# Query, key and value projections as seven half products per pair of feature blocks, with token sums streamed from DRAM

## The chip, the core and the metric

The kernel runs on one core of a Trainium2 chip. The metric is the device time of one execution in microseconds. TensorE (PE in the rows) multiplies matrices, VectorE (DVE), ScalarE (ACT) and GpSimd (POOL) do elementwise work, and SyncE (SP) issues the DMAs. Every engine works through its own instructions in order and waits on semaphores.

## What is computed

One decoder layer on 1040 tokens (16 learned ones ahead of 1024) of 1024 features. The part that matters here, cut from the reference:

```python
xn = rms_norm(h, mix_pre_g[l])
proj = xn @ w_in[l]                       # z, xbc, dt, q, k, v side by side
q = proj[..., OFF_Q:OFF_K].reshape(Bsz, L, SB_HEADS, SB_HEAD_DIM)
k = proj[..., OFF_K:OFF_V].reshape(Bsz, L, SB_HEADS, SB_HEAD_DIM)
v = proj[..., OFF_V:IN_COLS].reshape(Bsz, L, SB_HEADS, SB_HEAD_DIM)
y_ssd = ssd_mixer(z, xbc, dt_raw, ...)    # a scan over 9 chunks of tokens, 2 groups of heads
y_sb = rms_norm(stick_breaking_attention(q, k, v).reshape(Bsz, L, SB_WIDTH), sb_norm_g[l])
mix = jnp.concatenate([y_ssd, y_sb], axis=-1) @ w_out[l]
h = h + rms_norm(mix, mix_post_g[l])      # then the feed-forward part
```

q, k and v are 1024 features each: 16 heads of 64, taken as 8 pairs of heads, so 8 blocks of 128 features of each kind, 24 in all. Attention takes the pairs one after the other, and for each pair 8 blocks of 128 queries.

## The kernel before

The normed tokens lie transposed in SBUF, features on the partitions: `xs`, in three tiles by token columns (`CH`: 400, 384, 256), each with a high part (a 32-bit format that TensorE reads in one pass) and a low part, the rest. A weight block is loaded (`wr_`, 512 KB), ScalarE rounds it to the high part (`wh_`, L151), GpSimd subtracts for the low part (`wl_`, L152). `project_steps` (L165) then does, for each of three chunks of columns and eight blocks of 128 features, three matmuls: high by high, high by low, low by high. That is 72 matmuls for each of the 24 blocks of q, k and v. ScalarE takes q and v out of PSUM (L382, L394); k is split into high and low by ScalarE and VectorE (L388, L389).

These projections are filler. `qkv_flow` yields half chunks (12 matmuls, in the first pairs whole chunks of 24), and the code that runs the scan of the second group of heads (`scan_steps(1)`) and later the attention loop takes one to a few of them at hand-set places (`FILL`, `run(fill, ...)`). In attention TensorE's order is that of the code; the other engines' orders come from a scheduler. For pair p and query block i the loop does `block_weights` (scores `z` on TensorE, two sigmoids on ScalarE into `kp` and `bt`, a product scan over `kp` on VectorE, L773, the product of `bt` with it on GpSimd, L775), and, three blocks behind, `block_turn` (transposes `tw`, copied to `th`) and `block_mix` (`av`, the product with the values). `kp` has two buffers, `bt` three. PSUM has two banks for projections (`psum_mm`). All loads and stores stand in SP's one queue.

The feed-forward part already does its up-projection as seven half products per two blocks of features, in matmuls of 258 columns (L1304); there the sums on the token side stay in SBUF and those of the weights are made on GpSimd (L1264 to L1268).

Of the kernel before, what the change touches and what calls it, by code (L numbers as in the profile page):

```python
# [9 lines left out]
F32 = mybir.dt.float32  # L10
# [22 lines left out]
CH = [(0, 400), (400, 384), (784, 256)]  # L33
# [8 lines left out]
WB = 3  # L42
PPC = XB * 4 + XB + NFF * 3 + NFF + 8 + 8
# [10 lines left out]
def tile_layer(ctx: ExitStack, tc: tile.TileContext, x, meta, rows, parts,  # L54
# [37 lines left out]
    def const(shape, dt, name):  # L92
# [5 lines left out]
    identb = const([P, P], BF16, "identb")  # L98
    nc.vector.tensor_copy(identb, ident)
    ones = const([P, P], F32, "ones")  # L100
    nc.vector.memset(ones, 1.0)
    tri = const([P, P], F32, "tri")
    nc.gpsimd.affine_select(out=tri, in_=ones, compare_op=ALU.is_ge, fill=0.0,
                            base=0, pattern=[[1, P]], channel_multiplier=-1)
    low = const([P, P], F32, "low")
    nc.gpsimd.affine_select(out=low, in_=ones, compare_op=ALU.is_gt, fill=0.0,
                            base=0, pattern=[[-1, P]], channel_multiplier=1)
    lowr = const([P, P], F32R, "lowr")
    nc.vector.tensor_copy(lowr, low)
    maskb = const([P, P], BF16, "maskb")  # L110
    nc.vector.tensor_scalar(maskb, low, -NEG, NEG, op0=ALU.mult, op1=ALU.add)
# [25 lines left out]
    xsd = [dr.tile([NT + 1, P, 512], F32, name=f"xsd{g}", tag=f"xsd{g}") for g in range(2)]  # L137
    mvd = dr.tile([NM, 8, P], F32, name="mvd", tag="mvd")
# [17 lines left out]
    def project_steps(w, ncol, chunks, evac, name, halves_=False, skip=0):  # L156
        hi, lo = w
        for c0, n in chunks:
            s = skip if c0 == 0 else 0
            acc = psum_mm(f"pj_{name}_{c0}")  # L160
            for k in range(KB):
                if halves_ and k == KB // 2:
                    yield
                for j, (a, b) in enumerate(((hi, 0), (hi, 1), (lo, 0))):
                    mm(acc[:ncol, :n - s], a[:, k, :ncol], xs[c0][:, b, k, s:n],  # L165
                       start=(k == 0 and j == 0), stop=(k == KB - 1 and j == 2))
            evac(acc, c0 + s, n - s)
            yield
# [31 lines left out]
    def x_third(c0, name):  # L200
        n = dict(CH)[c0]
        return xp.tile([P, 2, KB, n], F32R, name=name, tag=f"x{c0}")

    xs = {c0: x_third(c0, f"xs{c0}") for c0, _ in CH}
# [12 lines left out]
    def dt_steps(hl):  # L217
        for c0, n in CH:
            acc = psum_mm(f"pj_dt_{c0}")
            for k in range(KB):  # L220
                for j in range(2):
                    mm(acc[:32, :n], hl[:, k, :], xs[c0][:, j, k, :n],
# [5 lines left out]
    with tc.tile_pool(name="pre", bufs=3, side="right") as pre, \  # L228
# [47 lines left out]
        def turn_x(i):  # L276
            c0, nr = spans[i]
            tps = []
            for hf in range(2):
# [6 lines left out]
                base = max(a for a, _ in CH if a <= c0)  # L286
                h, l = (xs[base][:, j, 4 * hf:4 * hf + 4, c0 - base:c0 - base + nr] for j in range(2))
                tps.append((tp, h, l))
            for tp, h, _ in tps:
                nc.scalar.activation(h, tp[:, :, :nr], AF.Copy)  # L290
            for tp, h, l in tps:
                nc.vector.tensor_tensor(l, tp[:, :, :nr], h.bitcast(F32), op=ALU.subtract)
# [55 lines left out]
    qkv_w = [(src[p], f"{nm}{p}") for p in range(8) for nm, src in (("q", w_q), ("k", w_k), ("v", w_v))]  # L348
    ready = {}

    def weights_of(name, ahead=0):
        n = [nm for _, nm in qkv_w].index(name) + ahead
        if n < len(qkv_w) and qkv_w[n][1] not in ready:
            src, nm = qkv_w[n]
            ready[nm] = load_w(src, P, nm)
        return ready.get(name)

    def qkv_block(name, evac, halves_):
        w = weights_of(name)
        for i, _ in enumerate(project_steps(w, P, CH, evac, name, halves_, M0 * (name[0] == "q"))):  # L360
            if halves_ and i == 1:
                weights_of(name, 1)
            yield
# [3 lines left out]
    def qkv_steps(p, post):  # L367
        q = rp.tile([P, L + 3], F32, tag="rq", name=f"q{p}", bufs=3)
        kh = rp.tile([P, L], F32R, tag="rk", name=f"kh{p}", bufs=3)
        later, vt_ = {}, []  # L370

        def values():
            v = rp.tile([P, NT + 1, P], F32, tag="rv", name=f"v{p}")
            vc = rp.tile([P, P], F32, tag="vc", name=f"vc{p}")
            heads[p][2:] = [v, vc]

        def low_k():
            later["kl"] = rp.tile([P, L], F32R, tag="rkl", name=f"kl{p}", bufs=2)
            heads[p] = [q, (kh, later["kl"]), None, None]

        def ev_q(acc, c0, n):
            nc.scalar.activation(q[:, c0:c0 + n], acc[:, :n], AF.Copy)  # L382

        def ev_k(acc, c0, n):
            if c0 == 0:
                low_k()
            kl = later["kl"]
            nc.scalar.activation(kh[:, c0:c0 + n], acc[:, :n], AF.Copy)  # L388
            nc.vector.tensor_tensor(kl[:, c0:c0 + n], acc[:, :n], kh[:, c0:c0 + n].bitcast(F32), op=ALU.subtract)  # L389

        def ev_v(acc, c0, n):
            if c0 == 0:
                vt_.append(rp.tile([P, L], F32, tag="rt", name=f"vt{p}", bufs=1))
            nc.scalar.activation(vt_[0][:, c0:c0 + n], acc[:, :n], AF.Copy)  # L394

        names = [(f"q{p}", ev_q), (f"k{p}", ev_k), (f"v{p}", ev_v)]
        if p < 7:
            for nm, ev in names:
# [1495 lines left out]
```

## Time and profile before

| what | value |
|---|---|
| median of 3 runs | 1734.75 us (1733.84 to 1738.6) |
| the profiled execution | 1735.83 us, span 1733.7 us |
| granted TensorE clock | 0.995 |
| TensorE busy | 1708.7 us (99%) |
| VectorE busy | 1114.4 us (64%) |
| ScalarE busy | 821.6 us (47%) |
| GpSimd busy | 858.3 us (50%) |
| moved by DMA | 173.87 MB |

A matmul's end is modelled and overlaps the next one's start, so what a matmul costs in a row of them is read from start to start. A busy share is an average over stages: the projections of q, k and v stand in two of them, the second scan and attention.

### The profile page before, as it was taken

The page shows a single profiled execution, that of the slowest core. Times are in us where ns is not written, and L with a number is a line of the kernel's source. Part 1 is how long each engine was busy: PE and PEld are TensorE (multiplying, and loading weights), DVE is VectorE, ACT ScalarE, POOL GpSimd, SP SyncE. Part 2 cuts the span into 40 slices and gives each one's busy share as a digit, 9 for nine tenths or more (in the row PEclk, how much of TensorE's full clock was granted, in tenths as well). Part 3 has the DMA queues.
Part 4 walks back from the last instruction along what each step waited for, and adds up shares of the span by engine and source line. Part 5 has one row for each costly group of instructions (what it writes and reads, how often), then busy time and mean ns, then how long its engine had stood idle before and what let it go on. Part 6 is the DMA issues. An engine that isn't in the chain of part 4 may idle for free. (4 is left out here: it accounts for less than half of the span.)

```text
span 1733.7 us, 28039 instructions
## 1 busy us (share of the span) xinstructions
PE 1708.7 (99%) x11230; PEld 1498.9 (86%) x11230; DVE 1114.4 (64%) x1230; ACT 821.6 (47%) x1370; POOL 858.3 (50%) x645
## 2 busy tenths in 40 slices
PE   7999999999999999999999999999999999999998
PEld 6999889888999998998687778999988888887886
DVE  5752964775676686668531457676666666758777
ACT  5423653545566566567553245433333333343544
POOL 4323663685566576555642124587766777400001
PEclk9999999999999999999999999999999999999999
DMA  4232343231011111112215544233332222395335
GB/s 163 58 113 97 101 130 104 67 104 38 26 38 37 38 31 33 38 50 86 82 50 172 175 165 136 63 117 96 110 100 92 92 91 92 114 330 188 104 112 180
DMA packets 90674, 173.87 MB, mean 100 GB/s; under 512 B 10704, under 2 KB 35816, under 8 KB 90544
## 3 DMA queue, kind: packets, MB, share of 16 engines
q1 hardware_dynamic: 90544, 172.08, 31.0%
q8 instruction: 88, 1.44, 0.3%
q14 instruction: 42, 0.34, 0.1%
HBM read 122.32 MB, written 49.73 MB: 99 GB/s over the span
## 5 line engine op out<-in xcount | busy, mean ns | idle before, releaser
L775 POOL TENSOR_TENSOR bt<-bt,kp 128x256 f32<-128x256 f32 (+7 forms) x128 | 213.2, 1684 | 184.5 <-DVE kp L773 147.7
L773 DVE TENSOR_TENSOR_SCAN kp<-kp,hold 128x272 f32<-128x272 f32 (+7 forms) x128 | 183.4, 1473 | 26.0 <-ACT kp L766 14.1
L1247 POOL TENSOR_TENSOR wlo<-wr,whi 128x1024 fp32r<-128x1024 f32 x43 | 106.2, 2479 | 38.0 <-ACT whi L1246 38.0
L1751 POOL TENSOR_TENSOR fms<-fms 128x1 f32<-128x1 f32 x8 | 2.7, 333 | 223.7 <-DMA ar<-fda 187.5
L766 ACT ACTIVATE kp<-z 128x288 f32<-128x288 f32 (+6 forms) x112 | 82.5, 737 | 52.2 <-PE z L765 27.9
L1246 ACT ACTIVATE whi<-wr 128x1024 fp32r<-128x1024 f32 x43 | 45.6, 1059 | 111.5 <-PE fX L1304 68.3
L165 PE MATMUL pj_v<-xs,wh_v 128*128 128x400 f32 (+2 forms) x384 | 94.9, 334 | 0.0
L1376 DVE SCALAR_TENSOR_TENSOR ga<-gr,pp,ga 128x1024 f32<-128x1024 f32 x44 | 72.3, 1643 | 34.9 <-ACT ga L1369 34.1
L165 PE MATMUL pj_k<-xs,wh_k 128*128 128x400 f32 (+2 forms) x384 | 94.4, 333 | 0.0
L789 ACT ACTIVATE th<-tw 128x1024 f32<-128x1024 f32 (+2 forms) x96 | 75.6, 816 | 38.5 <-PE tw L787 38.4
L165 PE MATMUL pj_q<-xs,wh_q 128*128 128x386 f32 (+2 forms) x384 | 93.8, 331 | 0.0
L165 PE MATMUL pj_X<-xs,wh_X 128*128 128x400 f32 (+2 forms) x384 | 93.1, 330 | 0.0
L1636 ACT ACTIVATE dh<-ar 128x512 fp32r<-128x512 f32 x77 | 48.5, 630 | 92.4 <-PE dnB L1714 44.7
L165 PE MATMUL pj_z<-xs,wh_z 128*128 128x386 f32 (+2 forms) x384 | 91.5, 326 | 0.0
L741 DVE CAST qh<-q 128x128 fp32r<-128x128 f32 x64 | 46.9, 734 | 67.1 <-PE z L765 66.7
L1637 DVE TENSOR_TENSOR dl<-ar,dh 128x512 fp32r<-128x512 f32 x77 | 53.2, 691 | 50.3 <-ACT dh L1636 47.5
L951 PE MATMUL mo<-woa,yh 128*128 128x512 f32 x256 | 85.2, 400 | 0.0
L767 ACT ACTIVATE bt<-z 128x288 f32<-128x288 f32 (+6 forms) x112 | 82.8, 740 | 0.0
L802 PE MATMUL av<-th,v 128*64 128x128 f32 x1152 | 78.1, 280 | 0.0
L787 PE MATMUL tw<-ident,bt 128*128 128x128 f32 x576 | 75.4, 274 | 0.0
L802 PEld LDWEIGHTS av<-th,v 128*64 128x64 f32 x1152 | 62.3, 138 | 14.0 <-issue 11.3
L787 PEld LDWEIGHTS tw<-ident,bt 128*128 128x128 f32 x576 | 65.5, 141 | 5.8 <-issue 2.7
(560 smaller groups left out, 5635.2 us busy)
## 6 DMA issues: line engine op xcount, KB each, us to landing
wr<-in_w_up SPq DMA_DIRECT2D x44, 512.0 KB
fds<-ga SPq DMA_DIRECT2D x44, 256.0 KB
b<-in_w_down SPq DMA_DIRECT2D x44, 256.0 KB
ar<-fds SPq DMA_DIRECT2D x44, 256.0 KB
fda<-ga SPq DMA_DIRECT2D x33, 256.0 KB
ar<-fda SPq DMA_DIRECT2D x33, 256.0 KB
yk<-yd SPq DMA_DIRECT2D x16, 512.0 KB
wor<-in_w_out SPq DMA_DIRECT2D x12, 512.0 KB
```

Of the source, the lines that this page charges most:

```text
L165: mm(acc[:ncol, :n - s], a[:, k, :ncol], xs[c0][:, b, k, s:n], start=(k == 0 and j == 0), stop=(k == KB - 1 and j == 2))
L766: nc.scalar.activation(kp[:, :, a:a + w], z[:, :, :w], AF.Sigmoid, scale=-QSCALE)
L767: nc.scalar.activation(bt[:, :, a:a + w], z[:, :, :w], AF.Sigmoid, scale=QSCALE)
L773: nc.vector.tensor_tensor_scan(kp[:, j][:, ::-1], kp[:, j][:, ::-1], hold[:, L - n:L][:, ::-1], 0.0, op0=ALU.mult, op1=ALU.max)
L775: nc.gpsimd.tensor_tensor(bt[:, j, 0:m], bt[:, j, 0:m], kp[:, j, 1:m + 1], op=ALU.mult)
L787: nc.tensor.transpose(tw[:, j, b, :], bt[:, j, c0:c0 + P], ident)
L789: nc.scalar.activation(th[:, :, :nb, :], tw[:, :, :nb, :], AF.Copy)
L802: mm(av[halves[j], :], v[:, kb, halves[j]], th[:, j, b, :], start=kb == 0, stop=kb == i)
L951: mm(acc, u[:, k, :], v[:, cs], start=(k == 0 and j == 0), stop=(k == 7 and j == 2))
L1247: nc.gpsimd.tensor_tensor(l, raw, h.bitcast(F32), op=ALU.subtract)
L1376: nc.vector.scalar_tensor_tensor(v, self.g[jj][:, :, i:i + 256], fconv_w[:, j, i:i + 1], v, op0=ALU.mult, op1=ALU.add)
L1637: sub(lo[:, k], raw, hi[:, k].bitcast(F32), op=ALU.subtract)
```

## The change

The 24 blocks are taken in 12 pairs (k and q, v and q, k and v, for two head pairs at a time). For a pair, the weights and the tokens are each cut into a two by two arrangement: two feature blocks by two halves of the 1024 input features, and two halves of the input features by two halves of the tokens (520 columns). Seven half products, with sums of the quarters as operands, replace the eight. Each is done for two column pieces of 260, so a pair of blocks takes 14 steps of 12 matmuls (4 feature blocks by 3).

- Weight sums and their split into high and low are made for each pair on GpSimd and ScalarE (`split_a`, `sums`, `split_s2`, `split_s34`, `split_s1`).
- Four token sums (t1 to t4) are needed. They are made once, by `x_sums`, during the first scan, split into high and low, and written to DRAM (`xt13`, `xt42`). For every pair of blocks they are read back in 8 units (each 4 by 520 columns of 4 bytes on 128 partitions, 1.065 MB) into a ring of two slots, which takes the place of that quarter of the tokens that no product reads alone. A unit is loaded when the one two before it has been used.
- Products are combined in PSUM and, on VectorE, in the destination tiles.
- The chunks of the other projections (X, z, B, C, dt) become 320, 400 and 320 columns; the 400 are read as two pieces of 200, since the tokens lie in halves of 520.
- The steps are handed out at other places: three in the first three query blocks of a head pair, two in the others. Constants of the scan are built later, and the slots for the output weights are taken from the token quarters.

```diff
-CH = [(0, 400), (400, 384), (784, 256)]
+CH = [(0, 320), (320, 400), (720, 320)]
+QKV = [(1, "a11", "b11", True), (2, "a12", "b21", False), (6, "s2", "t2", True), (5, "s1", "t1", True),
+       (3, "s4", "b22", False), (7, "s3", "t3", True), (4, "a22", "t4", False)]
...
+    def x_sums(k):
+        r1, r2 = (rp.tile([P, 2, HT], F32R, tag="rkl", name=f"xr{j}_{k}", bufs=3).bitcast(F32) for j in range(2))
+        for r, kk in ((r1, k), (r2, k + 4)):
+            nc.gpsimd.tensor_tensor(r, xq[:, kk, :, 0].bitcast(F32), xq[:, kk, :, 1].bitcast(F32), op=ALU.add)
+        nc.gpsimd.tensor_tensor(r1[:, 0], r1[:, 1], r1[:, 0], op=ALU.subtract)
+        nc.gpsimd.tensor_tensor(r1[:, 1], r2[:, 1], r1[:, 1], op=ALU.subtract)
...
+    def load_unit():
+        u = loaded[0]
+        if u < len(units):
+            loaded[0] += 1
+            (src, j), c = t_of[units[u][0]], units[u][1]
+            nc.sync.dma_start(out=ring[u % 2].bitcast(F32), in_=src[:, j, c].rearrange("p k b n -> p k (b n)"))
...
+        def split(self, raw, n1, n2):
+            hi, lo = self.slot(n1)
+            nc.scalar.activation(hi, raw, AF.Copy)
+            nc.gpsimd.tensor_tensor(lo, raw, hi.bitcast(F32), op=ALU.subtract)
+            self.w[n1], self.w[n2] = (hi[:, 0:4], lo[:, 0:4]), (hi[:, 4:8], lo[:, 4:8])
...
+        def sums(self):
+            r1, r2 = self.r
+            nc.gpsimd.tensor_tensor(r1[:, 0:4], r1[:, 0:4], r2[:, 0:4], op=ALU.subtract)
+            nc.gpsimd.tensor_tensor(r2[:, 0:4], r2[:, 0:4], r2[:, 4:8], op=ALU.add)
...
+        def step(self, s):
+            (n, wn, xn, first), c = QKV[s // 2], s % 2
...
+            if first:
+                self.acc[c] = psum_mm(f"pj{n}_{self.n}_{c}")
...
+            for k in range(4):
+                for j, (w, b) in enumerate(((hi, 0), (hi, 1), (lo, 0))):
+                    mm(acc[:, :HP], w[:, k, :], rv[:, k, b, :], start=first and k == 0 and j == 0,
+                       stop=k == 3 and j == 2, skip_group_check=not first)
+            if xn[0] == "t":
+                load_unit()
...
+            elif n == 6:
+                add(c21, a, c21, op=ALU.add)
+            elif n == 5:
+                add(c22, a, c21, op=ALU.add)
...
-            run(fill, 1 + (i < FILL[p]))
+            run(fill, 1 + (i < 3))
...
-            run(fill, int((p > 0 or i > 3) and (p, i) != (6, 6)))
+            run(fill, 1)
```

Two places show how the instructions move. First TensorE, in attention, between the scores of query blocks 2 and 3 of head pair 1 (`av0_7`: values product of pair 0, block 7; `tw1_0`: transposes of pair 1, block 0). Before, the tail of the key projection of pair 2 and the head of its value projection:

```order
L802 MATMUL av0_7_4863<-th0_7_1_4828,v0_3893 64x128 x8
L165 MATMUL pj_k2_784_4830<-xs784_135,wh_k2_4490 128x256 x2
L165 MATMUL pj_k2_784_4830<-xs784_135,wl_k2_4491 128x256
...
L787 MATMUL tw1_0_0_4895<-ident_69,bt1_0_4645 128x128 x2
L165 MATMUL pj_v2_0_4900<-xs0_133,wh_v2_4740 128x400 x2
L165 MATMUL pj_v2_0_4900<-xs0_133,wl_v2_4741 128x400
```

In the changed kernel, the fifth, sixth and seventh step of the block pair numbered 4 (`pj6`: the product with t2, once for each column piece; `pj5`: the one with t1; `xall` holds the tokens and the ring):

```order
L942 MATMUL av0_7_5254<-th0_7_1_5215,v0_3951 64x128 x8
L464 MATMUL pj6_4_0_5272<-xall_126,whis2_4_5012 128x260 x2
L464 MATMUL pj6_4_0_5272<-xall_126,wlos2_4_5013 128x260
...
L464 MATMUL pj6_4_1_5287<-xall_126,whis2_4_5012 128x260 x2
L464 MATMUL pj6_4_1_5287<-xall_126,wlos2_4_5013 128x260
...
L927 MATMUL tw1_0_0_5308<-ident_69,bt1_0_5029 128x128 x2
L464 MATMUL pj5_4_0_5313<-xall_126,whis1_4_5230 128x260 x2
L464 MATMUL pj5_4_0_5313<-xall_126,wlos1_4_5231 128x260
```

Two half chunks have become three steps, and the third reads a unit that is loaded into the slot that the first has left; between the two stand one step and two transposes.

Second GpSimd, in attention, from block 5 of head pair 2 on (`bt2_5`: the products of that block, `cb` their edge, `wl_` and `wlo` low parts of weights). Before:

```order
L775 TENSOR_TENSOR bt2_5_5767<-bt2_5_5767,kp2_5_5766 128x768 x2
L776 TENSOR_TENSOR cb2_5350<-bt2_5_5767,kp2_5_5766 128x2x15
L152 TENSOR_TENSOR wl_v4_6195<-wr_v4_6193,wh_v4_6194 128x1024
L775 TENSOR_TENSOR bt2_6_5841<-bt2_6_5841,kp2_6_5840 128x896 x2
L776 TENSOR_TENSOR cb2_5350<-bt2_6_5841,kp2_6_5840 128x2x15
L775 TENSOR_TENSOR bt2_7_5938<-bt2_7_5938,kp2_7_5937 128x1024 x2
```

And in the changed kernel:

```order
L915 TENSOR_TENSOR bt2_5_6258<-bt2_5_6258,kp2_5_6257 128x768 x2
L916 TENSOR_TENSOR cb2_5779<-bt2_5_6258,kp2_5_6257 128x2x15
L393 TENSOR_TENSOR wlos1_6_6354<-wr1_6_5883,whis1_6_6353 128x1024
L915 TENSOR_TENSOR bt2_6_6358<-bt2_6_6358,kp2_6_6357 128x896 x2
L916 TENSOR_TENSOR cb2_5779<-bt2_6_6358,kp2_6_6357 128x2x15
L393 TENSOR_TENSOR wloa11_7_6445<-wr0_7_6316,whia11_7_6444 128x1024
L401 TENSOR_TENSOR wr0_7_6316<-wr0_7_6316,wr1_7_6442 128x512
L402 TENSOR_TENSOR wr1_7_6442<-wr1_7_6442 128x512
L408 TENSOR_TENSOR s2_7_6702<-wr1_7_6442,wr0_7_6316 128x512
L410 TENSOR_TENSOR wr0_7_6316<-wr0_7_6316,s2_7_6702 128x512
L915 TENSOR_TENSOR bt2_7_6449<-bt2_7_6449,kp2_7_6448 128x1024 x2
```

Between the products of blocks 6 and 7, where nothing stood before, now stand five instructions of the weights.

More of the change, by code (lines that the diff above doesn't have):

```diff
@@ L97, in tile_layer @@
     make_identity(nc, ident)
[L98 to L111, printed above, removed]
+    one = const([P, 1], F32, "one")
+    nc.vector.memset(one, 1.0)
+    maskb = const([NM, NM], BF16, "maskb")
     nhalf = const([P, 16], F32, "nhalf")
@@ L346, in tile_layer @@
     heads, state = {}, {}
[L348 to L362, printed above, removed]
-            yield
```

317 lines of the change are left out of this document (214 added, 103 removed).

## The prediction

> **What bounds the kernel now.** I read the page's busy times first, then the windows of the stages that hold the projections (the second scan, attention, both together), and behind them the first scan and a piece of the feed-forward part.
>
> ```profile
> PE 1708.7 (99%) x11230; PEld 1498.9 (86%) x11230; DVE 1114.4 (64%) x1230; ACT 821.6 (47%) x1370; POOL 858.3 (50%) x645
> core 0: us, PE busy (x) PEld busy (x) DVE busy (x) ACT busy (x) POOL busy (x), PEclk, DMA share, GB/s
> 170.00:313.50 143.50, 143.03 (x948) 130.34 (x947) 100.20 (x103) 71.20 (x134) 78.95 (x63) 1.00 0.36 107
> 313.50:400.50 87.00, 87.00 (x577) 73.39 (x576) 62.62 (x83) 44.39 (x112) 66.60 (x61) 1.00 0.32 91
> 400.50:820.70 420.20, 417.15 (x3511) 378.36 (x3510) 291.12 (x305) 263.73 (x439) 251.79 (x204) 1.00 0.14 40
> 313.50:820.70 507.20, 504.15 (x4087) 451.75 (x4086) 353.74 (x388) 308.12 (x551) 318.39 (x264) 1.00 0.17 49
> 1200.00:1250.00 50.00, 50.00 (x339) 46.05 (x338) 32.41 (x29) 15.09 (x18) 38.12 (x22) 1.00 0.30 102
> ```
>
> PE is busy for 504.15 of the 507.20 us, at full clock. Whatever takes work from PE there shortens the time, as long as nothing else becomes late; whatever makes PE wait lengthens it by the wait. The second scan already has GpSimd at 66.6 of 87 us, attention has VectorE at 291 and GpSimd at 252 of 420, and the DMA engines are nearly idle (0.14).
>
> **TensorE's work.** A matmul's price is read from start to start in the timeline of PE; the last row is a step of the feed-forward part, 24 matmuls of 258 columns, from the chain.
>
> ```profile
> 503.17 0.52 PE L165 MATMUL pj_q<-xs,wh_q 128*128 128x384 f32 x2
> 503.71 0.51 PE L165 MATMUL pj_q<-xs,wh_q 128*128 128x384 f32 x2
> 504.23 0.51 PE L165 MATMUL pj_q<-xs,wh_q 128*128 128x384 f32 x2
> 512.06 0.40 PE L165 MATMUL pj_q<-xs,wh_q 128*128 128x256 f32 x2
> 512.41 0.40 PE L165 MATMUL pj_q<-xs,wh_q 128*128 128x256 f32 x2
> 1125.16 2.87 PE fA L1304 x24
> ```
>
> Three matmuls of 384 columns take 0.52 to 0.54 us, 0.174 to 0.18 each; three of 256 take 0.35, 0.117 each; one of 400 is by proportion 0.181. Each of the 24 blocks has 24 of each: 24 x 24 x (0.181 + 0.174 + 0.117) = 272 us. The feed-forward step gives 2.87 / 24 = 0.1196, so 0.1205 for 260 columns. Twelve pairs of blocks with 14 steps of 12 are 2016 matmuls, 243 us. The gain is **29 us**, an eighth of the products less an overhead for shorter matmuls. A step lasts 12 x 0.1205 = 1.45 us.
>
> **The ring.** Eight of the fourteen steps read a 1.065 MB unit from DRAM, and the load of a unit starts when the step two before it in the ring has ended. No load of that size is in the trace. The nearest is a weight block of 0.524 MB on an idle queue, with its issue (0.33 us) and what moved afterwards; the best sustained rate is in a stretch of loads behind attention.
>
> ```profile
> 610.92 0.33 SPq L150 DMA_DIRECT2D wr_q<-in_w_q  x1
> 612.40:613.40 1.00, 1.00 (x14) 0.74 (x12) 1.00 (x2) 0.51 (x1) 0.76 (x1) 1.00 0.75 299
> 613.40:614.40 1.00, 1.00 (x14) 0.83 (x15) 1.00 (x2) 1.00 (x3) 1.00 (x1) 1.00 0.39 156
> 614.40:615.40 1.00, 1.00 (x7) 1.00 (x7) 0.96 (x2) 1.00 (x3) 1.00 (x2) 1.00 0.00 0
> 936.80:951.40 14.60, 13.34 (x63) 10.76 (x65) 3.65 (x4) 6.40 (x7) 2.48 (x1) 1.00 0.94 324
> ```
>
> The block moves until within 613.4 to 614.4, so it takes 3.2 us, taking the middle of 2.5 and 3.5 with some completion. A unit has 0.541 MB more, at 324 GB/s another 1.67 us: **4.9 us** from a free slot to a usable one. Bounds: 4.0 (the load ended at the window's start, 2.5, and 1.67 less a little overlap of the loads in flight) and 5.5 (3.5 and other transfers in the way, weights of 1 MB per pair among them). The rate itself fits: 96 units x 3.3 us are 316 of some 480 us.
>
> The steps with products of t2 are numbers 4 and 5 of a pair, t1 6 and 7, t3 10 and 11, t4 12 and 13. Steps 4, 5, 10, 11 have four steps without a unit ahead of them and find theirs ready. Steps 6, 7, 12, 13 do not: between the end of step s-2 and the start of step s stand one other step, 1.45 us, and whatever attention work is dealt between. What that is worth comes from one stretch of PE's timeline.
>
> ```profile
> 501.55 1.25 PE L787 MATMUL tw<-ident,bt 128*128 128x128 f32 x10
> 502.56 0.59 PE L165 MATMUL pj_q<-xs,wh_q 128*128 128x384 f32 x2
> 505.28 0.43 PE L765 MATMUL z<-kh,qh 64*128 64x348 f32 x2
> 506.43 1.31 PE L802 MATMUL av<-th,v 128*64 128x128 f32 x20
> 507.67 0.62 PE L165 MATMUL pj_q<-xs,wh_q 128*128 128x384 f32 x2
> ```
>
> Ten transposes cost 1.01 us (0.1 each), six score matmuls of 348 columns 1.15, twenty value products 1.24 (0.062 each). At the place that the order shows (pair 4, step 4 to 6) there stand a step and two transposes, 1.45 + 0.2 = 1.65 us, so PE would wait 4.9 - 1.65, some 3.2 us. Where a whole block's transposes, scores and twenty value products stand as well, it is 1.45 + 1.0 + 1.15 + 1.24 = 4.85 us and nothing is left to wait. I priced the changed order this way over all 48 such steps, a wait of one pushing back the next load: 24 of them come up short, and the waits add to **29 us** at 4.9 us a load; at 4.0 they are 14, at 4.4 they are 22, at 5.5 they are 41. In the second scan the scan's own work lies between the steps, and the waits come out at zero.
>
> The Trainium skill ("DMA: Bandwidth & Descriptors", the anatomy of one DMA) fits a DMA as a fixed 2.0 us plus its bytes at 436 GB/s, a 4.44 us unit; the sum of waits would by that be 22 us instead of 29. The weight block would take 3.2 us by the same fit, which agrees with its rows; the sustained rate here, 324 GB/s, lies below the page's, and I go by the rows.
>
> The clock is the other thing a waiting PE can lose: in the one stretch where PE idled in this way the grant fell.
>
> ```profile
> 1020.00:1040.00 20.00, 18.08 (x86) 14.51 (x85) 10.39 (x11) 7.71 (x15) 4.75 (x8) 0.91 0.50 169
> ```
>
> With 1.9 of 20 us idle the grant is 0.91. The ring's waits are 3.2 us at the longest and apart from each other; I take 0 for this and up to 8 us in the range (0.09 of 48 steps of 1.45 us is 6.3, and a little around them). The Trainium skill ("TensorE: Matmul & The Clock Gate", what's actually happening) has the clock halved after an idle window of about 3.4 us: waits just under that would cost nothing, longer loads would cross it.
>
> **GpSimd and VectorE.** GpSimd makes the low parts and the sums. The prices are those of the same operations before and of the feed-forward part's sums; the wait row says what GpSimd was mostly waiting for in the two stages.
>
> ```profile
> L152 POOL TENSOR_TENSOR wl_k<-wr_k,wh_k 128x1024 fp32r<-128x1024 f32 x8 | 19.2, 2395 | 8.6 <-ACT wh_k L151 8.5
> L1264 POOL TENSOR_TENSOR wr<-wr 128x512 f32<-128x512 f32 x20 | 27.6, 1379 | 1.6
> L1265 POOL TENSOR_TENSOR wr<-wr,wr 128x512 f32<-128x512 f32 x20 | 29.7, 1483 | 1.6
> L1267 POOL TENSOR_TENSOR s<-wr,wr 128x512 f32<-128x512 f32 x19 | 29.1, 1532 | 0.0
> L1268 POOL TENSOR_TENSOR s<-wr,s 128x512 f32<-128x512 f32 x19 | 30.4, 1601 | 1.5
> POOL bt L775 <- DVE kp L773: 124.8, 43, 8.6
> L389 DVE TENSOR_TENSOR kl<-pj_k,kh x24: 398/558/576, 335.0 to 818.9; 128x400 fp32r<-128x400 f32 x8, 128x384 fp32r<-128x384 f32 x8, 128x256 fp32r<-128x256 f32 x8
> L1637 DVE TENSOR_TENSOR dl<-ar,dh 128x512 fp32r<-128x512 f32 x77 | 53.2, 691 | 50.3 <-ACT dh L1636 47.5
> ```
>
> A pair of blocks now costs three splits and five half-width operations: 3 x 2.4 + 1.4 + 1.5 + 1.5 + 1.6 + 1.3 = 14.4 us, where two blocks cost 2 x 2.4 = 4.8. Over twelve pairs GpSimd does 173 us in place of 57.5, **115 us more**. Three pairs' weights (43 us) fall into the second scan, in place of five blocks' (12): 66.6 + 31 = 97.6 us in a stage of 87. That stage then ends with GpSimd, about **+9 us**, less if the scan's own GpSimd work slides (0) or more if it stands behind it on the path (15). In attention 9 pairs are 130 us in place of 46: 252 + 84 = 336 of some 400 us. VectorE adds products into the destinations, ten operations per pair of 260 columns at about 0.40 us (the 256-wide minimum of the k row), 48 us in all and 36 in attention: 291 + 36 = 327. Both fit, at 82 to 84%, but a product of `bt` that comes up behind 5 us of weight work delays `tw`, and a split behind a `bt` product delays a step. I price the places where that catches PE at **+5 us** (0 to 15); work queued three blocks ahead covers the rest.
>
> **Edits that cost little.** `x_sums` stands in the first scan: per call on GpSimd two full adds and two half ones, 2 x 2.4 + 2 x 1.4 = 7.6 us, four times 31: 79 + 31 = 110 of 143.5. On VectorE per call two half operations and two full ones of twice 0.69: 16.6 in all, 100 + 17. Its DMA stores are 8.5 MB on a DMA share of 0.36. PE at 143.03 of 143.5 hides it; +2 (0 to 8), since the scan's own GpSimd steps stand behind these. The chunk widths leave columns and number of matmuls equal: 0, with 0 to 6 if a chunk read as two pieces of 200 is slower. SP's one queue is now passed by the units: a weight load or a unit that waits holds back all behind it, which is within the loads' upper bound above.
>
> **Sum.** -29 + 29 + 9 + 5 + 2 = **+16 us** against the profiled execution's 1735.83, so 1751.8; the median stands 1.1 below that execution, so 1750.7, and I say **1750**.
>
> **The rivals.** *The ring is hidden and GpSimd keeps up: faster.* If loads take 4.0 us or less and the scan's GpSimd work slides, the waits are at most 14 us, mostly under work that other engines would have delayed anyway, and the rest 0 to 2: -29 + 7 + 2 = -20, 1715 (1707 to 1729). For it: the feed-forward rows above do seven products with the same weight sums at PE 50.00 of 50 with GpSimd at 38, and only half of the tight steps have too little between. Against: there the token sums lie in SBUF, and the row of the weight block has 2.5 us at the least for half the bytes. It decides at about 29 - 16, so where the waits stay below 13 us. *GpSimd is the bound: much slower.* It waited 124.8 us for VectorE's product scan in these stages, because it works in order behind that scan. If this dependence stays as it is and does not shrink under the new work, GpSimd needs 318 - 58 + 173 = 433 us and 125 us of waits, 558 in place of 507; with PE's gain already in those 507 and half of the waits filled after all it is +45 at the middle, 1780. For it: the longest wait is 8.6 us, a whole block's turn. Against: the new work has no such partner and can fill these holes. It decides once more than 80 us of waiting remain. *It comes out even:* the ring costs 22 and GpSimd 7.
>
> **How the numbers follow.** Slower by the sum as above (from +6 up to +30): 0.42; GpSimd the bound: 0.12; faster: 0.36; within 0.3% (about 5 us, which is about what a measurement of this kernel can tell from no change): 0.10. The cases stand on both sides: the likeliest one's own range is 1741 to 1765. The range over all reaches from the full gain with small waits, 1708, to the sum of the upper bounds, -29 + 41 + 15 + 15 + 8 = +50, 1785.
>
> **What would show it.** Right: PE's idle time in the stages grows from 3 to some 30 us, and the waits ahead of the matmuls of `pj6`, `pj5`, `pj7` and `pj4` on `xall` are released by a DMA, up to 3.2 us each, at the second pair of units; the second scan ends with GpSimd at over 95%. The gain shows as 2016 matmuls at 0.1205. Wrong: units land within 4 us, or PE's idle stands before `tw` and `z` and is released by GpSimd, or a step takes well over 1.45 us from its first matmul to its last.

## The result and the profile after

The changed kernel takes **1863.57 us** (median of 4 runs, 1861.1 to 1864.13) against 1734.89 of the kernel before: a ratio of 1.0735, 95% interval 1.0716 to 1.0754. That is slower, as forecast, but by 129 us in place of 15, and outside the range (1708 to 1785). The profiled execution spans 1862.2 us.

The page's first part, of the kernel after:

```profile
PE 1728.9 (93%) x11518; PEld 1509.9 (81%) x11518; DVE 1211.4 (65%) x1376; ACT 841.9 (45%) x1396; POOL 1021.6 (55%) x733
```

PE is 93% busy in place of 99, and its busy time grew by 20 us although it multiplies less. The windows say where. First two stretches of before that were not shown yet (the work ahead of the first scan, and all that follows the attention loop's projections up to the feed-forward part):

```profile
60.00:153.90 93.90, 93.90 (x610) 92.38 (x609) 44.85 (x57) 30.67 (x55) 20.93 (x15) 1.00 0.29 91
820.70:1115.90 295.20, 291.01 (x1745) 232.88 (x1745) 146.73 (x154) 132.43 (x206) 107.26 (x94) 0.98 0.37 122
```

The same stretches of after, with the second scan and attention between them:

```profile
60.00:176.20 116.20, 103.47 (x629) 100.95 (x628) 69.28 (x75) 38.67 (x64) 50.72 (x29) 0.93 0.48 149
336.40:438.00 101.60, 92.69 (x680) 76.23 (x678) 81.52 (x109) 48.86 (x119) 90.28 (x73) 0.98 0.81 274
438.00:949.00 511.00, 427.61 (x3739) 384.45 (x3739) 348.81 (x413) 276.19 (x455) 356.69 (x261) 0.92 0.58 194
949.00:1244.50 295.50, 287.19 (x1697) 228.90 (x1696) 136.83 (x148) 128.15 (x197) 101.42 (x92) 0.99 0.36 122
```

Ahead of the first scan 22 us are lost (116 in place of 94), in the second scan 15 (101.6 in place of 87), in attention 91 (511 in place of 420), and nothing afterwards. In attention PE idles 83 us where it idled 3, and its granted clock is 0.92. The waits of PE in the kernel after:

```profile
PE pj L464 <- DMA xall<-xt: 49.1, 18, 9.6
...
PE z L905 <- ACT th L929: 9.3, 4, 4.1
PE tt_X L611 <- DVE xtk L607: 8.7, 4, 3.9
PE pj L464 <- DVE kl L443: 8.7, 6, 3.0
PE pj L464 <- POOL wlos L393: 5.8, 2, 3.7
```

The ring is the largest wait, 49.1 us in 18 waits, with the longest of 9.6. One such place, in the last pair, in the rows of SP, PE, GpSimd and VectorE:

```profile
902.20 0.33 SPq L1015 DMA_DIRECT2D wor<-in_w_out  x1
902.95 0.38 SPq L966 DMA_DIRECT2D yd<-ysc  x1
903.43 2.09 SPq L376 DMA_DIRECT2D xall<-xt  x2
...
909.29 2.34 POOL L973 TENSOR_TENSOR sq<-sq,sqb 128x1024 f32<-128x1024 f32 x1
...
909.45 2.33 DVE L882 TENSOR_TENSOR ql<-q,qh 128x128 fp32r<-128x128 f32 x1
...
911.76 0.77 PE L464 MATMUL pj<-xall,whis 128*128 128x260 f32 x2 [4.80 <-DMA xall<-xt]
...
912.54 0.64 PE L464 MATMUL pj<-xall,whis 128*128 128x260 f32 x2
...
913.19 0.64 PE L464 MATMUL pj<-xall,whis 128*128 128x260 f32 x2
...
919.39 0.29 DVE L882 TENSOR_TENSOR ql<-q,qh 128x128 fp32r<-128x128 f32 x1
```

The unit is issued at 903.43 and used at 911.76, 8.3 us later; a load and a store of 0.5 MB each were issued in the 1.2 us ahead of it, and a second unit right behind it (x2). The end of that wait in the windows, with the clock in the third column from the end, the DMA engines' share and GB/s behind it:

```profile
908.00:910.00 2.00, 0.00 (x0) 0.00 (x0) 1.97 (x3) 2.00 (x4) 2.00 (x3) 0.72 0.98 370
910.00:912.00 2.00, 0.24 (x1) 0.28 (x2) 2.00 (x2) 1.45 (x3) 1.64 (x1) 0.50 1.05 411
```

The DMA engines are full (0.98 and 1.05). And after 4.8 us of waiting PE's clock is at 0.50: three matmuls take 0.65 us (912.54 to 913.19) instead of 0.36, so part of the wait is paid again. The rows of VectorE hold the other half of the story, which the experiments led to: the same operation on 128 values takes 2.33 us while GpSimd runs beside it, ending about when GpSimd's does (911.78 and 911.63), and 0.29 us ten us later.

### The profile page after: what moved, and what is told of

Its sections match the earlier page's. It is cut to its first block, busy times and chain, and to the rows that moved or that the text cites. A ratio compares the mean times of both kernels' runs of the same rounds, so it can differ in the third digit from the quotient of the medians.

```text
span 1862.2 us, 29158 instructions
## 1 busy us (share of the span) xinstructions
PE 1728.9 (93%) x11518; PEld 1509.9 (81%) x11518; DVE 1211.4 (65%) x1376; ACT 841.9 (45%) x1396; POOL 1021.6 (55%) x733
## 5 line engine op out<-in xcount | busy, mean ns | idle before, releaser
L915 POOL TENSOR_TENSOR bt<-bt,kp 128x256 f32<-128x256 f32 (+7 forms) x128 | 213.4, 1686 | 146.6 <-DVE kp L913 114.4
L464 PE MATMUL pj<-xall,whis 128*128 128x260 f32 x960 | 203.1, 310 | 68.2 <-DMA xall<-xt 49.1
L464 PEld LDWEIGHTS pj<-xall,whis 128*128 128x128 f32 x960 | 158.9, 203 | 86.0 <-issue 52.4
L913 DVE TENSOR_TENSOR_SCAN kp<-kp,hold 128x272 f32<-128x272 f32 (+7 forms) x128 | 203.5, 1630 | 24.2 <-ACT kp L906 14.4
L464 PE MATMUL pj<-xall,wlos 128*128 128x260 f32 x480 | 143.4, 299 | 5.8 <-POOL wlos L393 5.8
L464 PEld LDWEIGHTS pj<-xall,wlos 128*128 128x128 f32 x480 | 97.9, 204 | 6.2 <-POOL wlos L393 6.2
L160 PE MATMUL pj_z<-xall,wh_z 128*128 128x306 f32 (+2 forms) x384 | 95.1, 335 | 0.0
L160 PE MATMUL pj_X<-xall,wh_X 128*128 128x320 f32 (+1 forms) x384 | 94.0, 330 | 0.0
L1084 PE MATMUL mo<-xall,yh 128*128 128x512 f32 x256 | 85.7, 402 | 0.0
L393 POOL TENSOR_TENSOR wlos<-wr,whis 128x1024 fp32r<-128x1024 f32 x24 | 64.5, 2686 | 37.2 <-ACT whis L392 37.2
L927 PE MATMUL tw<-ident,bt 128*128 128x128 f32 x576 | 80.1, 284 | 0.7 <-ACT bt L907 0.5
```

What stands on the lines that cost most here:

```text
L160: mm(acc[:ncol, :n - s], a[:, k, :ncol], x_cols(k, b, c0 + s, n - s), start=(k == 0 and j == 0), stop=(k == KB - 1 and j == 2))
L464: mm(acc[:, :HP], w[:, k, :], rv[:, k, b, :], start=first and k == 0 and j == 0, stop=k == 3 and j == 2, skip_group_check=not first)
L913: nc.vector.tensor_tensor_scan(kp[:, j][:, ::-1], kp[:, j][:, ::-1], hold[:, L - n:L][:, ::-1], 0.0, op0=ALU.mult, op1=ALU.max)
L915: nc.gpsimd.tensor_tensor(bt[:, j, 0:m], bt[:, j, 0:m], kp[:, j, 1:m + 1], op=ALU.mult)
L927: nc.tensor.transpose(tw[:, j, b, :], bt[:, j, c0:c0 + P], ident)
L1084: mm(acc, u[:, k, :], v[:, cs], start=(k == 0 and j == 0), stop=(k == 7 and j == 2))
```

## The experiments

Theory 1 was the forecast's own, larger: the stream of units. Theory 2 was that GpSimd's and VectorE's new work is the bound. The 74 us of waits on the ring that the expectations name are all the idle time ahead of the projections' matmuls, whatever ended it; the ring's own row is the 49.1 us shown above. Times are of one execution each where nothing else is said; the kernel before took 1735.6 to 1737.7 us beside them, and differences under 5 us are not read.

**once**: the ring is filled once.

```diff
         u = loaded[0]
-        if u < len(units):
+        if u < 2:
```

> The ring is filled once and never loaded again (the streaming is left out, the products read stale sums); token sums, weight sums, steps and additions stay. If the stream of units is what costs (theory 1), PE's waits on the ring (74 us in the changed kernel) and the lowered clock behind them (35 us at the most) go, and it takes 1755 to 1790 us. If GpSimd's and VectorE's new work is the bound (theory 2), the waits turn into waits for them and it stays over 1835.

1822.9 us, between the two bands: the stream costs 41 us, not 74 and more. With it gone, waits for VectorE come up:

```profile
PE pj L464 <- DVE kl L443: 11.3, 8, 2.8
...
PE pj L464 <- POOL wlos L393: 8.9, 2, 5.4
PE pj L464 <- DVE vt L485: 7.0, 3, 2.9
PE pj L464 <- DVE q L489: 6.9, 5, 2.2
```

But for the second row shown, where a low part of the weights comes late from GpSimd, these are steps that want an accumulator which VectorE has not emptied yet. Neither theory stands alone.

**once_nosums**: no unit is loaded, and no token sum is made.

```diff
-        if u < len(units):
+        if u < 0:
...
             run(fill, 1 + (i % 4 == 1))
-            if i % 4 == 3:
-                x_sums(i // 4)
```

> As with the ring filled once, and the four calls for the token sums with their stores are left out as well (the ring holds plain tokens). Theory: the token sums were moved ahead of the first scan by the scheduler and cost the 22 us by which that scan starts later (176 instead of 154); so this is 18 to 25 us faster than with the sums, with the first scan beginning at 154 to 156. Rival: the new chunk widths or the tokens' new layout cost those 22 us, and the first scan still begins at about 176.

1808.66 us, 14 us less than `once` and not the 18 to 25 of the theory, though the scan begins where the theory had it. The first scan's first matmuls (the first time in each row is where they begin), after and here:

```profile
L754 PE MATMUL sg<-sgh,lowr x36: 186/398/505, 176.2 to 421.1; 128*128 128x512 f32 x32, 16*16 16x64 f32 x4
```

```profile
L754 PE MATMUL sg<-sgh,lowr x36: 186/398/503, 154.5 to 401.3; 128*128 128x512 f32 x32, 16*16 16x64 f32 x4
```

The 22 us ahead of the first scan are the token sums', and chunk widths and layout cost nothing there. Some 7 of them are lost again behind it. The row of the sums' first operation, in the kernel after, shows why they stand there and not in the scan whose code calls them:

```profile
L354 POOL TENSOR_TENSOR xr<-xall x8: 2392/2428/3537, 31.5 to 135.1; 128x1040 f32<-128x1040 f32 x8
```

The last of the eight begins at 135.1 us, 41 us before the scan: the scheduler has put them there, while the tokens come in.

**few_pool**: the four half-width sums out, the splits kept.

```diff
-            nc.gpsimd.tensor_tensor(r1[:, 0:4], r1[:, 0:4], r2[:, 0:4], op=ALU.subtract)
-            nc.gpsimd.tensor_tensor(r2[:, 0:4], r2[:, 0:4], r2[:, 4:8], op=ALU.add)
...
-            nc.gpsimd.tensor_tensor(s2, r2[:, 4:8], r1[:, 0:4], op=ALU.subtract)
+            s2 = r2[:, 4:8]
             nc.scalar.activation(hi, s2, AF.Copy)
-            nc.gpsimd.tensor_tensor(r1[:, 4:8], r1[:, 4:8], s2, op=ALU.subtract)
```

> The stream stays, but the sums of the weights are left out: four half-width GpSimd operations per pair, 12 x 6 = 72 us of GpSimd work less (the products use plain quarters). Theory 1 (the stream): 1840 to 1863, since the ring's waits stay and only splits come earlier. Theory 2 (GpSimd is the bound): at least 40 us less, 1825 or below.

1851.16 us, 12 less for 72 us of GpSimd work: inside theory 1's band, but not nothing. The splits, the larger part of GpSimd's weight work, stayed.

**late_sums**: each sum first reads the state tile of the scan (`late[0] = prev` after each chunk's outputs).

```diff
         for r, kk in ((r1, k), (r2, k + 4)):
+            nc.gpsimd.tensor_tensor(r[:, 0, 0:1], late[0][:, 0:1], late[0][:, 0:1], op=ALU.add)
             nc.gpsimd.tensor_tensor(r, xq[:, kk, :, 0].bitcast(F32), xq[:, kk, :, 1].bitcast(F32), op=ALU.add)
```

> Everything is computed; each call for the token sums first reads the state that the first scan has reached, so the sums cannot be made before the scan. Theory: their cost ahead of the scan goes and the scan hides them, 1841 to 1848. Rival: they cost the scan as much as they cost ahead of it, 1858 to 1866.

1879.73 us, 16 *slower*, outside both bands. The first scan begins at 154.4, but PE then waits in it, 14.0 us in this row where the changed kernel has 4.0:

```profile
PE yt L818 <- DVE yo L789: 14.0, 5, 7.5
```

The sums cost more beside the scan, which waits for VectorE there. So the scheduler's place was the better of the two.

**no_adds**: from `once_nosums`, VectorE's additions and the low part of k out:

```diff
-            elif n == 6:
-                add(c21, a, c21, op=ALU.add)
-            elif n == 5:
-                add(c22, a, c21, op=ALU.add)
...
             elif n == 3:
-                add(self.part(0, 1, c), a, c21, op=ALU.add)
+                nc.scalar.activation(self.part(0, 1, c), a, AF.Copy)
...
             elif n == 4:
-                add(c21, a, c21, op=ALU.add)
+                nc.scalar.activation(c22, a, AF.Copy)
```

> No stream and no token sums, as in the kernel of 1808.7 us; in addition VectorE takes nothing out of PSUM any more (its ten additions per pair and the low part of k are left out; ScalarE copies the first, second, fourth and last product out). Theory 3: with two accumulators, PE's step waits for what VectorE still has to do with the step two before, and VectorE works in order behind the product scans of attention; then 40 to 55 us go, 1754 to 1770. Rival: the late low parts of the weights from GpSimd hold PE, and those waits come in place of the others: over 1790.

1782.3 us, 26 less, half of what was expected and in neither band: PE's waits for the low parts of the weights (`POOL wlos`) do come up, from 8.9 to 16.3 us, as the rival said. **no_adds_stream**, the same edit in the changed kernel with its stream:

> Stream, token sums and weight sums as in the changed kernel; only VectorE's additions and the low part of k are left out. If ring and accumulators cost one after the other, the same 40 to 55 us go as without the stream: 1808 to 1823. If the ring's waits cover those of the accumulators, it stays over 1840.

1841.81 us, 22 less. That is in the rival's band, but the bands had been made with a price that was too high: the additions cost 22 us with the stream and 26 without, so the two do not cover each other much.

**floor**: from `no_adds`, the weights' sums out as in `few_pool`, and every low part a copy by ScalarE.

```diff
             nc.scalar.activation(hi, raw, AF.Copy)
-            nc.gpsimd.tensor_tensor(lo, raw, hi.bitcast(F32), op=ALU.subtract)
+            nc.scalar.activation(lo, raw, AF.Copy)
```

> As without additions, and GpSimd has nothing to do for the projections either (no sums of weights; low parts are copies by ScalarE). What is left is PE's 2016 matmuls of 260 columns in their order. If the predicted price of PE's work was right, it is 29 us below the kernel before, less 4 us for more changes of operand: 1708 to 1718. If a step costs more than 1.45 us for a reason of its own, it is at 1725 or above.

1736.27 us, 46 less than `no_adds`, for GpSimd's weight work less what ScalarE's copies cost in its place, and no gain over before. It lies in the band that blamed PE's steps; whether it is they or ScalarE is tested next. **floor_act**, with high parts standing in for the low ones:

```diff
             nc.scalar.activation(hi, raw, AF.Copy)
-            nc.scalar.activation(lo, raw, AF.Copy)
-            self.w[n1], self.w[n2] = (hi[:, 0:4], lo[:, 0:4]), (hi[:, 4:8], lo[:, 4:8])
+            self.w[n1], self.w[n2] = (hi[:, 0:4], hi[:, 0:4]), (hi[:, 4:8], hi[:, 4:8])
```

> As the floor (no stream, no token sums, no additions, no GpSimd work for the weights), but the low parts of the weights are not made at all: the high parts stand in for them, so ScalarE loses the 42 copies of 1 us that the floor had given it. Theory: PE's shorter matmuls (25 us less by their starts in the floor's trace) were covered there by waits for ScalarE; without its copies the time falls to 1708 to 1722. Rival: attention's own chain from scores to transposes bounds once less filler stands in it, and the time stays at 1730 to 1737.

1721.59 us, at the upper edge of the first band: 15 us were ScalarE's copies (48 of them by the trace, not 42). PE's work in the projections by tile, before (q, k, v) and in `floor_act`:

```profile
300.00:925.00 625.00, 101.67 (x576) 90.00 (x576) 10.75 (x24) 1.00 0.17 51
300.00:925.00 625.00, 102.67 (x576) 90.95 (x576) 12.36 (x24) 11.06 (x24) 1.00 0.17 51
300.00:925.00 625.00, 103.64 (x576) 90.90 (x576) 11.08 (x24) 1.00 0.17 51
```

```profile
300.00:925.00 625.00, 278.55 (x2016) 252.16 (x2016) 46.75 (x128) 0.99 0.18 56
```

308.0 us have become 278.6: the predicted difference of 29 us is there. (Both are busy times, with modelled ends that overlap, so they stand above the prediction's 272 and 243.) The time is 14 us shorter.

**before_pool3** and **before_memset**: does GpSimd cost by its place in the order, or by what it reads? Both are the kernel before, with as much GpSimd work as the change adds, standing at nearly the same places in GpSimd's order:

```diff
+        for _ in range(3 if name[0] in "qkv" else 1):
             nc.gpsimd.tensor_tensor(lo[:, :, :ncol], raw[:, :, :ncol],
```

```diff
+        for _ in range(5 if name[0] in "qkv" else 0):
+            nc.gpsimd.memset(lo.bitcast(F32), 0.0)
         nc.gpsimd.tensor_tensor(lo[:, :, :ncol], raw[:, :, :ncol],
```

> The kernel before, with each of the 24 low parts of q, k and v made three times over by GpSimd: 48 more operations of 2.4 us, 115 us of GpSimd work, as much as the change adds. The prediction's price for that was 14 us (1750). Theory now, from the floor and the kernel without additions (46 us apart): the new work stands in GpSimd's order ahead of attention's products and slows VectorE's scans, 25 to 50 us (1760 to 1786).

> The kernel before, with five fills of each low part by GpSimd ahead of the subtraction: 120 memsets of about 1.0 us (0.32 us for 256 values, by proportion), 115 to 120 us of GpSimd work that reads nothing. If GpSimd's order is what costs, it takes as long as with three subtractions. If the cost is that GpSimd's reading holds VectorE's operations with two operands (scans grow from 1473 to 1776 ns in the kernel without additions), it stays within 10 us of the kernel before and the scans at about 1470 ns.

1767.15 us and 1738.16 us: the subtractions cost 32 us, the fills 3, at 115 us of GpSimd time each (48 of 2.4 us at their price before; the fills by their own rows, 120 of 0.96). The subtractions are stretched too: by their own rows the 72 come to 207.5 us, 2.5 to 3.2 us each. VectorE's product scan (128 of them, mean ns behind the busy time) in the kernel before, with subtractions and with fills:

```profile
L773 DVE TENSOR_TENSOR_SCAN kp<-kp,hold 128x272 f32<-128x272 f32 (+7 forms) x128 | 183.4, 1473 | 26.0 <-ACT kp L766 14.1
```

```profile
L774 DVE TENSOR_TENSOR_SCAN kp<-kp,hold 128x272 f32<-128x272 f32 (+7 forms) x128 | 224.6, 1795 | 21.7 <-issue 10.9 <-ACT kp L767 10.6
```

```profile
L775 DVE TENSOR_TENSOR_SCAN kp<-kp,hold 128x272 f32<-128x272 f32 (+7 forms) x128 | 184.6, 1482 | 20.8 <-ACT kp L768 10.5 <-issue 9.4 <-POOL wl_k L153 0.2
```

1473 ns before, 1795 with three subtractions, 1482 with fills: in this pair of kernels it is GpSimd's reading that holds VectorE's operations with two operands, and not the order. The Trainium skill ("SBUF — State Buffer", who interferes with whom) states this: a VectorE instruction with two inputs in SBUF contends with a GpSimd instruction that reads SBUF and not with one that only writes it. The scans' means here and the 2.33 us above agree.

**weights_vector**: all eight operations of `Blocks` a pair, one of them as an example.

```diff
-            nc.gpsimd.tensor_tensor(lo, raw, hi.bitcast(F32), op=ALU.subtract)
+            nc.vector.tensor_tensor(lo, raw, hi.bitcast(F32), op=ALU.subtract)
```

> Everything is computed; the sums and low parts of the weights are made by VectorE in place of GpSimd (12 x (3 x 1.38 + 5 x 0.69) = 91 us more for VectorE, 173 less for GpSimd). If GpSimd's order and its reading are what costs, 15 to 35 us go (1829 to 1849). If VectorE's queue is the scarce place, because PE's accumulators wait for it, it becomes slower than the changed kernel, 1870 or above.

1836.43 us, 27 less, inside the first band, though VectorE got some 90 us more to do. The scan's row there:

```profile
L913 DVE TENSOR_TENSOR_SCAN kp<-kp,hold 128x272 f32<-128x272 f32 (+7 forms) x128 | 177.5, 1427 | 24.7 <-ACT kp L906 14.8 <-issue 9.4
```

**all_vector** has `nc.vector` for `nc.gpsimd` in `x_sums` as well, **all_vector_queue** in addition the edit below, and **all_vector_once** instead of it the edit of `once`.

```diff
                 if s == 5 and nxt:
-                    nxt.load(1)
                     nxt.split_a()
-                if s == 8 and nxt:
+                if s == 7 and nxt:
+                    nxt.load(1)
+                if s == 9 and nxt:
                     nxt.sums()
```

> Everything is computed; weights' sums and low parts by VectorE as in the kernel of 1836.4 us, and the token sums' four GpSimd operations a call by VectorE too. If the 22 us ahead of the first scan come from GpSimd reading while VectorE works, 8 to 15 us go (1821 to 1828). If they come from VectorE's order (copies of transposed tokens queued behind the sums), it stays at 1832 to 1842.

> As the kernel with all of it on VectorE, and the second weight block of the next pair is loaded two steps later and its sums made one step later, so that no unit of the ring stands behind a weight load that waits for a buffer. In the changed kernel 16 of the ring's 74 us of waits were such late issues. If SP's order is a part of the stream's cost of its own, 8 to 16 us go against the kernel with all on VectorE. If the bytes in flight are what makes units late, less than 4.

> As the kernel with all of it on VectorE (1821.3 us), and the ring is filled once and never loaded again (the streaming is left out). If the stream's price is its own, the 41 us that it cost beside GpSimd's work go again or more, since VectorE's contention hid a part of it: 1765 to 1782. If it only stood in for waits on PE's accumulators, which come up in its place, less than 25 us go: over 1796.

1821.31, 1830.23 and 1783.12 us. Moving the token sums gives 15 more, inside the first band, and the first scan begins at 160.8 in place of 176.8. The later weight load did what it was to do to the ring, whose waits in `all_vector` and then in `all_vector_queue` are

```profile
PE pj L464 <- DMA xall<-xt: 50.6, 21, 6.2
```

```profile
PE pj L464 <- DMA xall<-xt: 34.6, 16, 6.2
```

16 us less, and yet it is 9 us slower, outside both bands: 6 of these stand ahead of the first scan (166.5 in place of 160.8), which the edit does not touch by itself, and in attention what the ring gave went to other waits. Which of them the later sums caused stays open. `all_vector_once` lies 1 us above its first band: the stream costs 38 us here as well, so its price does not hang on who makes the weights' and token sums.

**half_units**: from the third load on only two of a unit's four parts.

```diff
-            nc.sync.dma_start(out=ring[u % 2].bitcast(F32), in_=src[:, j, c]...)
+            h = 4 if u < 2 else 2
+            nc.sync.dma_start(out=ring[u % 2][:, 0:h].bitcast(F32), in_=src[:, j, c, 0:h]...)
```

> Everything of the changed kernel, but each load after the first two brings only half of its unit (0.53 MB in place of 1.065; the rest of the slot is stale). If the bytes in flight make a unit late, the ring's 74 us of waits fall below 20 and the time comes to within 15 us of the kernel that never loads again (1823): 1820 to 1838. If the fixed part of a load or the order of SP's queue does it, it stays above 1845.

1841.31 us, between the bands: half of the bytes give 22 of the stream's 41 us back, and the wait for the ring falls from 49.1 to 31.3:

```profile
PE pj L465 <- DMA xall<-xt: 31.3, 12, 8.2
```

**before_vector**: the kernel before with the low parts of q, k and v on VectorE.

```diff
-        nc.gpsimd.tensor_tensor(lo[:, :, :ncol], raw[:, :, :ncol],
+        (nc.vector if name[0] in "qkv" else nc.gpsimd).tensor_tensor(lo[:, :, :ncol], raw[:, :, :ncol],
```

> The kernel before, with the 24 low parts of q, k and v made by VectorE in place of GpSimd: 57 us of GpSimd work with two operands read go, VectorE gets 24 x 1.4 = 33 us more. By the run with three subtractions (115 us of such work cost 31.6 us) this is worth up to 15 us, but the kernel before keeps PE busy for 504 of 507 us in these stages, so no more than 3 to 5 us can come back: 1729 to 1734. Rival: VectorE's queue, with k's low parts and the scans in it, delays PE, 1737 to 1745.

1735.54 us (median of 10 runs) against 1736.84 (of 13), ratio 0.9995 (0.9983 to 1.0007): no change, between the two bands. Where PE is busy for 504 of 507 us there is next to nothing to give back. No kernel with everything computed beat the one before.

## Why the prediction was right and wrong

The runs make a ladder from the kernel before to the changed one, each step against the one above it:

| step | from, to | measured | predicted |
|---|---|---|---|
| PE's shorter work (and no low parts by GpSimd and VectorE) | before 1735.6, floor_act 1721.6 | -14 | -29 |
| GpSimd's weight work | floor_act, no_adds 1782.3 | +61 | +14 with the additions |
| VectorE's additions, low part of k | no_adds, once_nosums 1808.7 | +26 | in the 14 |
| token sums | once_nosums, once 1822.9 | +14 | +2 |
| stream | once, after 1863.6 | +41 | +29 |

The sum is +128. A step's price depends on what is already there, and the first one also leaves out low parts that the kernel before makes, so the 61 is the price of all 173 us of GpSimd's weight work and not only of the 115 added; `before_vector` suggests that the other 57.5 cost little.

**The step that failed** is the one on GpSimd and VectorE: 336 and 327 us of some 400 "fit, at 82 to 84%", with +5 in attention and +9 in the scan. It added each engine's work to that engine alone. In this ladder the two cost 61 and 26 us, together 87, not 14. What the runs show in place of the step is that the two engines hold each other up: GpSimd's reading stretches VectorE's operations with two operands (`before_pool3` against `before_memset`), among them the scan behind which attention's products, transposes and scores wait, and PE waits for accumulators that VectorE has not emptied (`once`, `no_adds`). By proportion to `before_pool3`, 32 us for 115, the 173 us of weight work would cost 48 by this reading (an estimate); how the rest of the 87 divides between it, VectorE's longer queue and GpSimd's order is not shown. The trace of before had the row for it:

```profile
L742 DVE TENSOR_TENSOR ql<-q,qh 128x128 fp32r<-128x128 f32 x64 | 41.8, 655 | 1.9
```

A mean of 655 ns for what takes 0.29 us alone (the row at 919.39) means that more than half of the time of this operation was waiting, in a kernel that already had GpSimd at 318 us in these stages. By its single rows 48 of the 64 take 0.29 us; the other 16 all run beside a GpSimd operation with two operands and end about when it does. There are 32 such in `before_pool3` and 11 in `weights_vector`. With the fills there are 25, and these too end with a two-operand operation and not with a fill.

In the scan's stage the +9 became 15, with GpSimd at 90.28 of 101.6 us: it is busy for 89%, not over 95, so it did not simply fill that stage; what made the 15 is not shown.

**PE's work**: right in busy time, 29.4 us. Only half of it reaches the time: in `floor_act` PE idles 12 us more than before, most of it in attention, with less filler there; the wait that grew most is the row below, 1.9 us before. In the changed kernel the clock behind the waits took the gain back: the projections' tile row there is 298.95 us at a clock of 0.93 against 278.55 at 0.99, 20 us where 0 was taken and 8 allowed. The ratio of the clocks alone would give 18 of them (an estimate).

```profile
PE z L890 <- ACT th L914: 6.3, 2, 5.8
```

And the tile row of the kernel after:

```profile
300.00:949.00 649.00, 298.95 (x2016) 267.36 (x2016) 62.36 (x152) 24.65 (x64) 0.93 0.60 201
```

**The ring**: the mechanism was right (the waits stand ahead of the ring's steps, released by a DMA, at the second pair of units, and none in the second scan), the term was mis-sized: 41 us, with 49.1 us of waits, for 29. A unit with nothing just ahead of it is used 5.1 to 5.9 us after its issue, little over the 4.9 of the prediction, here with a second one right behind it (x2):

```profile
821.07 1.81 SPq L376 DMA_DIRECT2D xall<-xt  x2
...
826.26 0.48 PE L464 MATMUL pj<-xall,whis 128*128 128x260 f32 x2 [3.55 <-DMA xall<-xt]
```

5.2 us. With one weight block of 0.5 MB issued 0.5 us ahead of it

```profile
477.28 0.34 SPq L385 DMA_DIRECT2D wr<-in_w_q  x1
477.73 0.37 SPq L376 DMA_DIRECT2D xall<-xt  x1
...
484.48 0.48 PE L464 MATMUL pj<-xall,whis 128*128 128x260 f32 x2 [3.04 <-DMA xall<-xt]
```

it takes 6.8. Of seven such places with one transfer of 0.5 MB just ahead, six have 5.9 to 6.8 and one has 8.3; the place shown first, with two ahead, has 8.3. The prediction's estimate by the Trainium skill ("DMA: Bandwidth & Descriptors", the anatomy of one DMA), 4.44 us, used a fit that the section gives for DMAs issued by GpSimd. The units here stand in SP's queue, and 5.1 us is the least seen where PE waited for one. The second weight load of the next pair is issued at just this point of a pair, step 5, so the first unit of t1 mostly stands behind it. The prediction put other transfers into its upper bound, 5.5, and not into the sum.

The longest wait, 9.6 where 3.2 was the longest predicted, has another cause, one that ties the ring to GpSimd:

```profile
794.66 2.48 POOL L393 TENSOR_TENSOR wlos<-wr,whis 128x1024 fp32r<-128x1024 f32 x1
...
797.17 0.34 SPq L385 DMA_DIRECT2D wr<-in_w_q  x1
797.62 0.92 SPq L376 DMA_DIRECT2D xall<-xt  x2
```

The unit's slot was free at 790.8, but in SP's one queue it stood behind a weight load that waited for GpSimd to be done with the buffer, and GpSimd made that low part only behind two products of `bt`. So the unit was issued 6.8 us late. Here GpSimd's order costs, by way of SP's queue; the prediction had counted a held queue as covered by the loads' upper bound. `all_vector_queue` takes such late issues away and is no faster, so what they cost in time is not shown.

**The token sums**: +2 was wrong, because the prediction took their place from the code. The trace has them ahead of the scan, where nothing hides them.

**Right**: the chunk widths at 0, and the sign, by the likeliest case: its added terms, the ring, the two engines and the token sums, point the right way and are all too small. Two sums of the prediction do not come out. Its upper bound, +50, leaves out the 8 us for the clock or the token sums and the 6 for the chunks; with them it is +64, still far below what was measured. And the rival with GpSimd as the bound, 1780 at 0.12, has +45 with half of GpSimd's 125 us of waits filled, where 433 and 62 are 495 of 507 us, no loss at all. That rival had the right engine and a wrong mechanism: GpSimd's waits for the scan are not what grew (its row on the page went from 147.7 to 114.4 us); the scans themselves grew. Their group in the kernel after:

```profile
L913 DVE TENSOR_TENSOR_SCAN kp<-kp,hold 128x272 f32<-128x272 f32 (+7 forms) x128 | 203.5, 1630 | 24.2 <-ACT kp L906 14.4
```

The mean is 1630 ns, 1473 before.

## What to carry to other kernels

Before GpSimd is given work because it is half idle, compare the mean of VectorE's short two-operand operations with their shortest: where they are stretched, more work for one engine costs the other time, even if both have room. Price a streamed operand by what stands ahead of it in its queue when it is asked for, waiting loads included, and not by its own load alone; and beside a wait of PE of several us count the clock after it, here some 20 us in all. Take the place of an instruction from the order that the scheduler made, not from the line that calls it.

## What was not expected of the hardware

- GpSimd subtractions of 115 us cost 32 us of time and stretch VectorE's scans from 1473 to 1795 ns; as much time in GpSimd fills costs 3 us and leaves them at 1482 ns.
- A load of 1.065 MB is used 5.2 us after its issue with a second one right behind it, after 5.9 to 6.8 us, once 8.3, with 0.5 MB just ahead of it, and after 8.3 with 1 MB ahead: what is ahead counts, with the engines at 370 to 411 GB/s in the last case, and what is behind counts little.
- After a wait of 4.8 us PE's clock is at 0.50 for some us (in the window shown), and three matmuls of 260 columns take 0.65 in place of 0.36 us.
